# Feed-forward up products of a three-block kernel as 2x2 block products in seven multiplications, activations through DRAM

## Chip, core and metric

The kernel runs on one core of one Trainium2 chip. The metric is the device time of one execution in microseconds (us); the time of the kernel before is the median of three runs. All tensors are float32 in DRAM.

## The reference, cut to what matters

Three transformer blocks follow each other on 1024 tokens of width 1024. The first and the second end in a gated feed-forward of inner width 2816 (2730 padded up to a multiple of 256), and that is all the change touches.

```python
def first_block(x, ...):
    ...
    h = h + merged @ w_out[l]
    hn = rmsnorm(h, norm_ffn[l])
    g, up = jnp.split(hn @ w_ffn_in[l], 2, axis=-1)
    h = h + (jax.nn.silu(g) * up) @ w_ffn_out[l]
    return rmsnorm(h, norm_final)

def _hybrid_layer(x, p_i, ...):
    ...
    x = _layer_norm(ALPHA * x + mix, ln1_g, ln1_b)
    gate_ff, up_ff = jnp.split(x @ w_ffn_in, 2, axis=-1)
    ffn = (jax.nn.silu(gate_ff) * up_ff) @ w_ffn_out
    ple = jax.nn.sigmoid(x @ w_ple_gate) * (p_i @ w_ple_proj)
    return _layer_norm(ALPHA * x + ffn + ple, ln2_g, ln2_b)
```

## The kernel before

Every large product is made of three matmuls: a float32 operand is kept as two fp32r parts, hi (a rounded copy) and lo (the rest), and `mm3` (L89 to L95) issues hi by hi, hi by lo and lo by hi, each a 128x128 stationary block by 512 columns. `weight` (L78 to L88) brings one weight tile: SP starts the load of w_raw (128x1024, 512 KB), DVE casts w_hi (L86), POOL subtracts w_lo (L87).

`ffn` (L370 to L412) is called once in the first block ("ffn1") and once in the second ("ffn2"). The inner width is cut into F_TILES = 22 tiles of 128. `up(fi)` loads the gate and the up weights of a tile and makes, for each half of the tokens (hf, 512 columns), a gate product and an up product of 24 matmuls each (`fm`: 8 slices of the width by 3). ACT takes the Silu (L380), DVE multiplies (L381), ACT copies act_hi (L383), DVE subtracts act_lo (L384); the activations stay in SBUF. `down` (L387 to L397) adds, for a group of two tiles, their part of the down product to the residual h: for each of 8 token tiles t and 2 column halves n one PSUM tile of 2 x 3 = 6 matmuls, then a DVE addition into h (L395). The groups are nine of two and a last one of four (LAST = 4). The loop at L400 to L409 interleaves them: the first up tile of a group, the down products of the group before, the second up tile. With the last group the hook `done` runs the norm of each finished token tile and the start of the next block.

The order on each engine is that of the program text as a scheduler of the tile framework arranges it by priorities and buffer waits; a tile that gets a buffer waits for the last reader of what lay there. PSUM gives these products three tiles in turn: two tagged mm and one tagged mf; transposes have two more (tr). h is eight tiles of 128x1024 in SBUF through the whole feed-forward. x_fm are the inputs with the width on the partitions, hi and lo, for the two token halves; they lie in SBUF units of a ring (12 units in the first block; in the second one ring of 8 and one of 4). The norm that makes x_fm (L170 scales a row tile, PE transposes it at L156, ACT copies hi at L135, DVE subtracts lo at L137) is still at work on the second token half when the first feed-forward begins. In the second block a gated product ("ple") stands ahead of the feed-forward; DVE multiplies (L1040) and POOL adds it to h (L1042).

## Time and profile before

| | |
|---|---|
| median of three runs | 3527.93 us (3527.26 to 3531.14) |
| the profiled execution's own time | 3537.72 us |
| its span, first to last instruction | 3536.0 us |
| mean granted TensorE clock | 0.974 |
| PE busy | 3367.1 us (95%), 15456 matmuls and transposes in the records |
| DVE, ACT, POOL busy | 1896.1 (54%), 877.4 (25%), 1048.1 us (30%) |
| feed-forward stages | about 716 to 1463 us and 2118 to 2859 us |

The page is of one execution, so times of stretches are compared with 3537.72 us and not with the median. The names in it: PE is the matmul engine, PEld its weight loads, which run beside it, DVE the vector engine, ACT the scalar engine, POOL the GpSimd engine, SP the engine that issues most loads. A matmul's own row shows the time from its start to its modelled end, and matmuls overlap; how long one takes of PE's time is read from the number of them in a stretch. "[3.49 <-DVE hm L931]" behind a row is idle time of that engine just before it and what ended it.

### The profile page before, as it was taken

Reading aid. Unit: us, or ns where it says so; the run is one execution under the profiler, and the core shown is the slowest. Engines: PE = TensorE matmul, PEld = TensorE weight load, DVE = VectorE, ACT = ScalarE, POOL = GpSimd, SP = SyncE. Lnnn points to the kernel's source line nnn. Section 1 sums busy time; section 2 is a strip of 40 time slices with the busy share of each in tenths; the row PEclk is TensorE's granted clock in tenths of the full one; section 3 lists DMA queues with packets and bytes.
Section 4 is the critical chain, followed back from the end, with each engine's and each line's share of the span. In section 5 each row is a group of like instructions: output and inputs, shape, how many; then the busy total and the mean of one; then the engine's idle time right before and its main releaser. Section 6 shows DMA issues by size and latency. Waiting matters only on the chain. (4 is left out here: it accounts for less than half of the span.)

```text
span 3536.0 us, 39137 instructions
## 1 busy us (share of the span) xinstructions
PE 3367.1 (95%) x15456; PEld 2750.8 (78%) x15456; DVE 1896.1 (54%) x3048; ACT 877.4 (25%) x1694; POOL 1048.1 (30%) x618
## 2 busy tenths in 40 slices
PE   8999999999999999999979899999999986889998
PEld 6888888888888888778768788888888865667776
DVE  5455457343333333657768843334334379985665
ACT  3333311110000000312245520000000133445552
POOL 3111122132222222133444452222222366552221
PEclk9999999999999999999989999999999988999899
DMA  4111124221111111222251121111111221122241
GB/s 137 65 62 62 57 63 132 95 60 45 52 48 48 48 48 54 78 84 90 85 185 49 36 77 56 54 50 44 54 49 42 72 81 36 42 93 78 76 143 66
DMA packets 88359, 247.13 MB, mean 70 GB/s; under 512 B 13120, under 2 KB 18368, under 8 KB 88176
## 3 DMA queue, kind: packets, MB, share of 16 engines
q1 hardware_dynamic: 60176, 194.60, 17.4%
q10 hardware_dynamic: 27952, 49.91, 4.3%
q8 instruction: 121, 1.98, 0.2%
q14 instruction: 62, 0.51, 0.0%
q0 software_dynamic: 48, 0.13, 0.0%
HBM read 204.17 MB, written 40.69 MB: 69 GB/s over the span
## 5 line engine op out<-in xcount | busy, mean ns | idle before, releaser
L87 POOL TENSOR_TENSOR w_lo<-w_raw,w_hi 128x1024 fp32r<-128x1024 f32 x267 | 657.1, 2462 | 1891.1 <-DVE w_hi L86 1434.0
L86 DVE CAST w_hi<-w_raw 128x1024 fp32r<-128x1024 f32 x259 | 235.6, 910 | 468.6 <-PE mm L94 272.3
L93 PE MATMUL mm<-x,w_hi 128*128 128x512 f32 x696 | 284.5, 409 | 23.5 <-DVE kl L277 10.5
L94 PE MATMUL mm<-x,w_hi 128*128 128x512 f32 x696 | 283.2, 407 | 0.0
L95 PE MATMUL mm<-x,w_lo 128*128 128x512 f32 x696 | 280.5, 404 | 1.9 <-POOL w_lo L87 1.9
L93 PE MATMUL mf<-x,w_hi 128*128 128x512 f32 x568 | 229.1, 403 | 12.4 <-DVE u L1126 11.5
L95 PE MATMUL mf<-x,w_lo 128*128 128x512 f32 x568 | 225.2, 396 | 1.2 <-POOL w_lo L87 1.2
L94 PE MATMUL mf<-x,w_hi 128*128 128x512 f32 x568 | 225.8, 397 | 0.0
L395 DVE TENSOR_TENSOR h<-h,mm 128x512 f32<-128x512 f32 x210 | 143.9, 686 | 116.8 <-PE mm L95 116.5
L94 PE MATMUL mm<-h,w_hi 128*128 128x512 f32 x512 | 199.5, 390 | 0.2 <-DVE h L137 0.2
L93 PE MATMUL mm<-h,w_hi 128*128 128x512 f32 x512 | 199.4, 389 | 0.1
L95 PE MATMUL mm<-h,w_lo 128*128 128x512 f32 x512 | 199.2, 389 | 0.0
L93 PE MATMUL mm<-w_hi,act_hi 128*128 128x512 f32 x462 | 183.6, 398 | 0.0
L94 PE MATMUL mm<-w_lo,act_hi 128*128 128x512 f32 x462 | 182.9, 396 | 0.0
L95 PE MATMUL mm<-w_hi,act_lo 128*128 128x512 f32 x462 | 182.8, 396 | 0.0
L383 ACT ACTIVATE act_hi<-sg 128x512 fp32r<-128x512 f32 x88 | 55.7, 632 | 505.6 <-DVE sg L381 499.6
L93 PEld LDWEIGHTS mm<-x,w_hi 128*128 128x128 f32 x696 | 135.0, 194 | 57.1 <-issue 23.5
L95 PE MATMUL mm<-y,w_lo 128*128 128x512 f32 x448 | 174.3, 389 | 0.0
L94 PE MATMUL mm<-y,w_hi 128*128 128x512 f32 x448 | 174.3, 389 | 0.0
L93 PE MATMUL mm<-y,w_hi 128*128 128x512 f32 x448 | 174.3, 389 | 0.0
L381 DVE TENSOR_TENSOR sg<-sg,mm 128x512 f32<-128x512 f32 x64 | 43.7, 684 | 238.7 <-PE mm L95 237.5
L1140 DVE SCALAR_TENSOR_TENSOR cy<-u,cols,cy 128x1024 f32<-128x1024 f32 x80 | 166.2, 2083 | 0.9
(430 smaller groups left out, 7837.7 us busy)
## 6 DMA issues: line engine op xcount, KB each, us to landing
w_raw<-in_w_ffn_in_dram SPq DMA_DIRECT2D x88, 512.0 KB, 3.6
w_raw<-in_w_in_dram SPq DMA_DIRECT2D x78, 512.0 KB, 3.6
w_raw<-in_w_ffn_out_dram SPq DMA_DIRECT2D x44, 512.0 KB, 3.5
w_raw<-in_w_out_dram SPq DMA_DIRECT2D x24, 512.0 KB, 3.7
gates_d<-go SPq DMA_DIRECT2D x32, 256.0 KB, 2.0
gt<-gates_d ACTq DMA_DIRECT2D x32, 256.0 KB, 3.5
x_d<-h SPq DMA_DIRECT2D x16, 512.0 KB, 2.6
xt<-in_x_dram SPq DMA_DIRECT2D x8, 512.0 KB, 8.4
```

Source lines behind the costliest of these rows:

```text
L86: nc.vector.tensor_copy(hi, raw)
L87: nc.gpsimd.tensor_tensor(out=lo, in0=raw, in1=f(hi), op=ALU.subtract)
L93: mm(out_, lh, rh, start=start and i == 0, stop=False)
L94: mm(out_, lh, rl, start=False, stop=False)
L95: mm(out_, ll, rh, start=False, stop=stop and i == n - 1)
L381: tt(out=sg, in0=sg, in1=u, op=ALU.mult)
L383: act(out=at[0][:, c], in_=sg, func=AF.Copy)
L395: tt(out=h, in0=h, in1=pt, op=ALU.add)
L1140: stt(out=y, in0=src, scalar=w, in1=y, op0=ALU.mult, op1=ALU.add)
```

## The change

The up products and the down products are taken apart: all 22 up tiles come first, their activations (float32, before the split) go to a DRAM buffer act_d, and then all down products run, which load them again (L549), copy the hi part on ACT (L550) and subtract the lo part on DVE (L551). h is written to DRAM before the up products (ACT's queue, L532) and read again before the down products (ACT's queue, L570); the space of h is used by the pool "up" in between.

Twenty of the 22 up tiles are made as a 2x2 block product in seven multiplications. The four blocks of a weight tile pair are (gate, up) by (first, second half of the width); the four blocks of the input are (first, second half of the width) by (first, second half of the tokens). Each multiplication is four slices of the width by three matmuls, 12 matmuls, so a tile has 84 in place of 96. Seven weight operands per tile are prepared: three blocks as they are and four sums and differences (s1 on POOL, s2, s4, s3 on DVE, L462); ACT copies the hi part of each (L448), POOL subtracts the lo part (L449). They are prepared AHEAD = 6 operands ahead of their product. On the input's side t1, t3, t2 and a new b12 are made once per feed-forward (`sums`, `last_sums`; L391, L396, L402, L405, L407, L415). The results are put together on DVE (L507, L514, L515, L518, L523) from PSUM tiles pa, pd (the mm pair) and pb, pc (own banks, one buffer each). The first two tiles are made in the plain way, the second token half first, while `sums` runs in between.

In the first block the activations of the first groups are loaded into the same ring of 12 units that holds x_fm, t1 and t3; in the second into the ring of 4. The diff, cut (the calls in the two blocks pass the rings, a DRAM tile for h and a function that opens h's pool again):

```diff
-    def mm3(out_, terms, start=True, stop=True):
+    def mm3(out_, terms, start=True, stop=True, onto=False):
...
+    def silu_mul(pl, g, u, dst, c):
+        sg = pl.tile([P, HS], F32, name="sg", tag="sg", bufs=2)
+        act(out=sg, in_=g, func=AF.Silu)
+        tt(out=dst[:, c], in0=sg, in1=u, op=ALU.mult)
...
+    def ffn_up(pl, pp, unit, unit_r, x_fm, w_in, act_d, plain=2):
...
+        half_k = lambda h, k: tuple(fm_.at[4 * k][0] for fm_ in x_fm[h])
+        b11, b21, b12, b22 = half_k(0, 0), half_k(0, 1), half_k(1, 0), half_k(1, 1)
+        t1, t3 = (tuple(four(unit(f"{n}{j}")) for j in range(2)) for n in ("t1", "t3"))
+        t2 = tuple(four(unit_r(f"t2{j}")) for j in range(2))
+        dve, pool_e = nc.vector.tensor_tensor, nc.gpsimd.tensor_tensor
...
+        def whole(n, x, k, eng):
+            o = tmp(n)
+            eng(out=o, in0=f(x[0][:, k]), in1=f(x[1][:, k]), op=ALU.add)
+            return o
+        def parts(x, k, src, eng):
+            act(out=x[0][:, k], in_=src, func=AF.Copy)
+            eng(out=x[1][:, k], in0=src, in1=f(x[0][:, k]), op=ALU.subtract)
+        def sums():
+            for k in range(4):
+                x11, x12, x22 = whole("p1", b11, k, pool_e), whole("u2", b12, k, dve), whole("u3", b22, k, pool_e)
+                dve(out=x11, in0=x12, in1=x11, op=ALU.subtract)
+                parts(t1, k, x11, pool_e)
+                yield
+                dve(out=x12, in0=x22, in1=x12, op=ALU.subtract)
+                parts(t3, k, x12, pool_e)
+                dve(out=x22, in0=x22, in1=x11, op=ALU.subtract)
+                parts(t2, k, x22, dve)
+                yield
...
+        def last_sums():
+            for k in range(4):
+                x21, y2 = whole("p1", b21, k, pool_e), whole("u2", t2, k, dve)
+                dve(out=x21, in0=x21, in1=y2, op=ALU.subtract)
+                parts(b12, k, x21, pool_e)
...
+            return ao, lambda h: nc.sync.dma_start(act_d[fi][:, sl[h]], ao[:, sl[h]])
+        gen = sums()
+        for fi in range(plain):
             wg, wu = weight(w_in[fi]), weight(w_in[F_TILES + fi])
...
+            ao, store = out_of(fi)
+            for h in (1, 0):
+                g = fm(wg, x_fm[h])
+                u = fm(wu, x_fm[h])
+                silu_mul(pl, g, u, ao, sl[h])
+                store(h)
+                for _ in range(2 if fi < plain - 1 or h else 8):
+                    next(gen, None)
+        n_op, held = [0], []
...
+        def operand(src, eng):
+            hi, lo = slot()
+            nc.scalar.copy(hi, src)
+            eng(out=lo, in0=src, in1=f(hi), op=ALU.subtract)
+            return hi, lo
+        def operands(fi):
+            raw = []
+            for j in (F_TILES + fi, fi):
+                r = wp.tile([P, 1024], F32, name="w_raw", tag="w_raw", bufs=2)
+                nc.sync.dma_start(r, w_in[j])
+                raw.append(r)
+            (a21, a22), (a11, a12) = ((r[:, 0:512], r[:, 512:1024]) for r in raw)
+            def mix(x, y, op, eng):
+                s = pl.tile([P, 512], F32, name="s", tag="s", bufs=4)
+                eng(out=s, in0=x, in1=y, op=op)
+                return s
+            yield operand(a11, pool_e)
+            s1 = mix(a21, a22, ALU.add, pool_e)
+            yield operand(s1, pool_e)
+            s2 = mix(s1, a11, ALU.subtract, dve)
+            yield operand(s2, pool_e)
+            s4 = mix(a12, s2, ALU.subtract, dve)
+            s3 = mix(a11, a21, ALU.subtract, dve)
+            yield operand(a12, pool_e)
+            yield operand(s3, pool_e)
+            yield operand(a22, pool_e)
+            yield operand(s4, pool_e)
...
+        AHEAD = 6
+        xs = (b11, t1, t2, b21, t3, b12, b22)
...
+        more(AHEAD)
+        last_sums()
...
+            def product(i, pt, start=True):
+                w = ready.pop(0)
+                mm3(pt, [(kslice(w, k), tuple(x[:, k] for x in xs[i])) for k in range(4)], start, onto=not start)
+            pa, pd = mmtile("mm", 2), mmtile("mm", 2)
+            pb, pc = (pp.tile([P, HS], F32, name=n, tag=n, bufs=1) for n in ("pb", "pc"))
+            p1, u2, u3 = tmp("p1"), tmp("u2"), tmp("u3")
+            product(0, pa)
+            act(out=p1, in_=pa, func=AF.Copy)
+            more(1)
+            product(1, pc)
+            more(1)
+            product(2, pb)
+            tt(out=u2, in0=p1, in1=pb, op=ALU.add)
+            more(1)
+            product(3, pa, False)
+            sg = tmp("sg")
+            act(out=sg, in_=pa, func=AF.Silu)
+            more(1)
+            product(4, pb, False)
+            tt(out=u3, in0=p1, in1=pb, op=ALU.add)
+            tt(out=p1, in0=u3, in1=pc, op=ALU.add)
+            more(1)
+            product(5, pd)
+            tt(out=u3, in0=u3, in1=pd, op=ALU.add)
+            tt(out=ao[:, sl[0]], in0=sg, in1=u3, op=ALU.mult)
+            store(0)
+            more(1)
+            product(6, pc, False)
+            tt(out=u2, in0=u2, in1=pc, op=ALU.add)
+            act(out=u2, in_=u2, func=AF.Silu)
+            tt(out=ao[:, sl[1]], in0=u2, in1=p1, op=ALU.mult)
+            store(1)
+            more(1)
...
+    def ffn(x_fm, unit, unit_b, h, h_d, h_st, open_h, w_in, w_out, before_last, done, group=2):
+        act_d = dram.tile([F_TILES, P, S], F32, name="act_d")
+        for t in range(NT):
+            nc.scalar.dma_start(h_d[t * P:(t + 1) * P], h[t])
+        h_st.close()
+        with ExitStack() as c:
+            pool("up_edge", side="right", c=c).tile([P, 24], F32, name="edge")
+            unit_r = units(pool("up_t2", side="right", c=c), 2)
+            ffn_up(pool("up", side="right", c=c), pool("up_ps", space=PSUM, c=c), unit, unit_r, x_fm, w_in, act_d)
+        open_h()
+        with ExitStack() as c:
+            pool("down_edge", side="right", c=c).tile([P, 24], F32, name="edge")
+            dp = pool("down", side="right", c=c)
...
+            def load(fi, last):
+                if last:
+                    hi, lo = (dp.tile([P, S], F32R, name=f"act_{j}", tag=f"act_{j}", bufs=LAST) for j in ("hi", "lo"))
+                else:
+                    at = unit_b("act")
+                    hi, lo = at[:, 0:S], at[:, S:2 * S]
+                nc.sync.dma_start(f(lo), act_d[fi])
+                act(out=hi, in_=f(lo), func=AF.Copy)
+                nc.vector.tensor_tensor(out=lo, in0=f(lo), in1=f(hi), op=ALU.subtract)
+                return hi, lo
...
+            def down(fis, ats, done=None):
...
+                        pt = mmtile()
+                        mm3(pt, [(tuple(x[:, t * P:(t + 1) * P] for x in at), kslice(w, n, 512))
+                                 for at, w in zip(ats, ws)])
+                        hh = h[t][:, n * 512:(n + 1) * 512]
+                        tt(out=hh, in0=hh, in1=pt, op=ALU.add)
...
+            groups = [list(range(g, g + group)) for g in range(0, F_TILES - LAST, group)]
+            groups.append(list(range(F_TILES - LAST, F_TILES)))
+            ats = [[load(fi, False) for fi in groups[0]]]
             for t in range(NT):
...
+                nc.scalar.dma_start(h[t], h_d[t * P:(t + 1) * P])
+            for i, fis in enumerate(groups[:-1]):
+                nxt_g = groups[i + 1]
+                ats.append([load(fi, nxt_g is groups[-1]) for fi in nxt_g])
+                down(fis, ats[i])
+            before_last()
+            down(groups[-1], ats[-1], done)
+            done.flush()
```

PE at the start of the first feed-forward, before (mg is the merged input of the projection, h_5194 and h_5196 are hi and lo of the first token half, tr a transpose of the norm xn):

```order
3179 L94 MATMUL mm<-w_lo,mg_4547 128x512
3180 L95 MATMUL mm<-w_hi,mg_4549 128x512
3181 L93 MATMUL mf<-h_5194,w_hi 128x512 [waits DVE_49,Activation_49]
3182 L93 MATMUL mm<-h_5194,w_hi 128x512 [waits DVE_49]
3183 L156 MATMUL tr<-sq_c,xn 128x128 [waits DVE_49,PE_49]
3184 L156 MATMUL tr<-sq_c,xn 128x128 x3
3185 L94 MATMUL mf<-h_5196,w_hi 128x512
3186 L95 MATMUL mf<-h_5194,w_lo 128x512 [waits Pool_49]
```

The same place after (h_5198 is hi of the second token half):

```order
3193 L158 MATMUL tr<-sq_c,xn 128x128 [waits DVE_49]
3194 L158 MATMUL tr<-sq_c,xn 128x128 x3
3195 L158 MATMUL tr<-sq_c,xn 128x128 [waits DVE_49]
3196 L158 MATMUL tr<-sq_c,xn 128x128 x3
3197 L95 MATMUL mf<-h_5198,w_hi 128x512 [waits Activation_49]
3198 L95 MATMUL mm<-h_5198,w_hi 128x512
3199 L95 MATMUL mm<-h_5194,w_hi 128x512
3200 L96 MATMUL mm<-h_5196,w_hi 128x512
```

Up products of the first token half stood between the transposes of the second half; now the first product comes after all transposes, and is of the second half.

DVE after, where the first feed-forward goes from its last Strassen tile to the down products (L514 to L525 put that tile together, L551 are the lo parts of loaded activations, L562 the additions into h):

```order
957 L514 TENSOR_TENSOR u_8876<-p_8874,pb 128x512 [waits PE_49]
958 L551 TENSOR_TENSOR act<-act 128x1024 [waits DMAHW2_49,Activation_49]
959 L515 TENSOR_TENSOR p_8874<-u_8876,pc 128x512 [waits DVE_49]
960 L551 TENSOR_TENSOR act<-act 128x1024 [waits DMAHW3_49,Activation_49]
961 L518 TENSOR_TENSOR u_8876<-u_8876,mm 128x512 [waits DVE_49,PE_49]
962 L551 TENSOR_TENSOR act<-act 128x1024 [waits DMAHW4_49,Activation_49]
963 L519 TENSOR_TENSOR ao<-sg,u_8876 128x512 [waits DVE_49]
964 L551 TENSOR_TENSOR act<-act 128x1024 [waits DMAHW5_49,Activation_49]
965 L523 TENSOR_TENSOR u_8875<-u_8875,pc 128x512 [waits PE_49]
```

Nothing of before answers to it; there the additions into h stand between those of up tiles. Five more of L551 and L525 follow, then the first L562 (row 971).

ACT after, at the same place (L550 are the hi copies of loaded activations, L524 the last Silu, L570 the loads of h):

```order
649 L550 ACTIVATE act<-act 128x1024 [waits DMAHW6_49,PE_49]
650 L524 ACTIVATE u_8875<-u_8875 128x512 [waits DVE_49,Activation_49]
651 L550 ACTIVATE act<-act 128x1024 [waits DMAHW0_49,PE_49]
652 L550 ACTIVATE act<-act 128x1024 [waits DMAHW2_49,PE_49]
653 L550 ACTIVATE act<-act 128x1024 [waits DMAHW3_49,PE_49]
654 L570 DMA h_8983<-h_d 128x1024 [waits Pool_49]
655 L570 DMA h_8984<-h_d 128x1024 [waits DMAHW1_49]
```

The loads of h stand behind the copies of all activations that the ring of 12 takes. In all, PE's order of after has 480 matmuls less than that of before.

## Rows read from the trace of the kernel before

**Rows 1.** The page, engines: busy us (share of the span), instructions.
```profile
PE 3367.1 (95%) x15456; PEld 2750.8 (78%) x15456; DVE 1896.1 (54%) x3048; ACT 877.4 (25%) x1694; POOL 1048.1 (30%) x618
```

**Rows 2.** Stretches of both feed-forwards: length, busy per engine (instructions), clock, DMA share, GB/s.
```profile
800.00:900.00 100.00, 100.00 (x438) 81.97 (x438) 35.94 (x46) 7.38 (x12) 22.79 (x10) 1.00 0.16 48
...
1300.00:1400.00 100.00, 100.00 (x440) 82.25 (x439) 31.18 (x39) 8.89 (x15) 20.18 (x9) 1.00 0.15 43
...
2100.00:2200.00 100.00, 100.00 (x441) 82.27 (x440) 31.43 (x37) 11.06 (x17) 29.92 (x14) 1.00 0.18 53
...
2700.00:2800.00 100.00, 100.00 (x440) 82.23 (x439) 32.08 (x41) 8.61 (x14) 21.58 (x9) 1.00 0.19 60
```

**Rows 3.** Groups of instructions on feed-forward lines: busy us, mean ns, idle before.
```profile
L395 DVE TENSOR_TENSOR h<-h,mm 128x512 f32<-128x512 f32 x210 | 143.9, 686 | 116.8 <-PE mm L95 116.5
L383 ACT ACTIVATE act_hi<-sg 128x512 fp32r<-128x512 f32 x88 | 55.7, 632 | 505.6 <-DVE sg L381 499.6
```

**Rows 4.** Lines of POOL and DVE: minimum, median, maximum ns, first and last start.
```profile
L1042 POOL TENSOR_TENSOR h<-h,sg x16: 1282/1292/1735, 2045.6 to 2121.7; 128x512 f32<-128x512 f32 x16
L87 POOL TENSOR_TENSOR w_lo<-w_raw,w_hi x267: 2344/2397/3383, 22.9 to 3500.5; 128x1024 fp32r<-128x1024 f32 x134
L86 DVE CAST w_hi<-w_raw x259: 659/694/2822, 21.8 to 3499.7; 128x1024 fp32r<-128x1024 f32 x130
L384 DVE TENSOR_TENSOR act_lo<-sg,act_hi x88: 691/1144/1893, 736.5 to 2801.3; 128x512 fp32r<-128x512 f32 x88
```

**Rows 5.** DMA issues: count, KB each, median us from issue to landing.
```profile
w_raw<-in_w_ffn_in_dram SPq DMA_DIRECT2D x88, 512.0 KB, 3.6
...
x_d<-h SPq DMA_DIRECT2D x16, 512.0 KB, 2.6
...
h<-in_x_dram ACTq DMA_DIRECT2D x8, 512.0 KB, 7.8
```

**Rows 6.** Start us, duration us, instruction: a DVE operation beside one of POOL, and alone.
```profile
2993.70 3.36 DVE L1140 SCALAR_TENSOR_TENSOR cy<-u,cols,cy 128x1024 f32<-128x1024 f32 x1
...
2993.63 2.35 POOL L1146 TENSOR_TENSOR y<-y,pr 128x1024 f32<-128x1024 f32 x1 [1.26 <-ACT pr L1145]
...
3014.70 1.27 DVE L1140 SCALAR_TENSOR_TENSOR cy<-u,cols,cy 128x1024 f32<-128x1024 f32 x1
```

**Rows 7.** Start of the first feed-forward: a stretch, and two DVE rows.
```profile
720.00:740.00 20.00, 18.75 (x94) 14.92 (x93) 9.37 (x13) 6.59 (x10) 5.27 (x3) 1.00 0.23 72
...
717.24 0.67 DVE L581 TENSOR_TENSOR h<-h,mm 128x512 f32<-128x512 f32 x1
...
732.59 1.29 DVE L137 TENSOR_TENSOR h<-tr,h 128x512 fp32r<-128x512 f32 x2 [0.78 <-ACT h L135]
```

**Rows 8.** 128x1024 operations of ACT and DVE with SBUF operands: minimum, median, maximum ns.
```profile
L165 ACT ACTIVATE junk<-h x32: 1043/1060/1069, 682.9 to 3528.8; 128x1024 f32<-128x1024 f32 x32
...
L170 DVE SCALAR_TENSOR_TENSOR xn<-h,rstd,gain x8: 1272/1283/1287, 684.9 to 727.7; 128x1024 f32<-128x1024 f32 x8
```

**Rows 9.** PE after a gap in the second block, timeline, and the stretch's clock.
```profile
1748.73 0.77 PE L922 MATMUL co<-vt,W 128*128 128x129 f32 x2 [3.49 <-DVE hm L931]
...
1753.16 0.63 PE L94 MATMUL mf<-x,w_hi 128*128 128x512 f32 x1
1753.59 0.63 PE L95 MATMUL mf<-x,w_lo 128*128 128x512 f32 x1
...
1750.00:1755.00 5.00, 5.00 (x21) 4.55 (x21) 3.95 (x16) 2.09 (x8) 2.01 (x2) 0.55 0.29 112
```

**Rows 10.** A stretch at the program's start, when loads come in a burst.
```profile
10.00:12.00 2.00, 1.01 (x5) 1.01 (x6) 1.55 (x2) 1.15 (x2) 1.36 (x1) 1.00 1.07 415
```

More of the change, by code (lines that the diff above doesn't have):

```diff
@@ L559, in block1, with open_h @@
         att_stack.close()
-        hp_ = pool("h1", side="right", c=mp)
-        h = [hp_.tile([P, D], F32, name=f"h{t}") for t in range(NT)]
+        h, h_st = [], ExitStack()
+        def open_h(c=mp):
+            hp_ = pool("h1", side="right", c=c)
+            h[:] = [hp_.tile([P, D], F32, name=f"h{t}") for t in range(NT)]
+        open_h(h_st)
         h_fm = new_fm("h1")
@@ L596, in block1 @@
                       *(lambda t, fn=fn: fn(t, h[t], nxt[0], nxt[1][0]) for fn in finish))
-        with ExitStack() as c:
-            fp = pool("ffn1", side="right", c=c)
-            ffn(fp, h_fm, h, a["w_ffn_in"], a["w_ffn_out"], before_last, done)
+        ffn(h_fm, unit, unit, h, dram.tile([S, D], F32, name="h1_d"), h_st, open_h, a["w_ffn_in"], a["w_ffn_out"],
+            before_last, done)
         mp.close()
@@ L995, in block2, with open_h @@
         unit("low")
-        hp_ = pool("h2", side="right", c=hs)
-        h = [hp_.tile([P, D], F32, name=f"h{t}") for t in range(NT)]
+        h, h_st = [], ExitStack()
+        def open_h(c=hs):
+            hp_ = pool("h2", side="right", c=c)
+            h[:] = [hp_.tile([P, D], F32, name=f"h{t}") for t in range(NT)]
+        open_h(h_st)
         mix = gqa(unit, unitb, h, ple, at)
@@ L1045, in block2 @@
                       *(lambda t, fn=fn: fn(t, h[t], nxt[0], nxt[1][0]) for fn in finish))
-        with ExitStack() as c:
-            fp = pool("ffn2", side="right", c=c)
-            ffn(fp, x_fm, h, a["w_ffn_in_2"], a["w_ffn_out_2"], before_last, done)
+        ffn(x_fm, unit, unitb, h, dram.tile([S, D], F32, name="h2_d"), h_st, open_h, a["w_ffn_in_2"],
+            a["w_ffn_out_2"], before_last, done)
         hs.close()
```

72 lines of the change are left out of this document (33 added, 39 removed).

## Prediction

> **What bounds the kernel now.** I read the busy shares first, then the table of stretches, the rows of the feed-forward lines, and last the places where two engines meet. PE is busy 95% of the span; DVE, ACT and POOL have large gaps [rows 1]. Inside both feed-forward stages there is nothing but PE: each of four 100 us stretches shows PE at 100.00 with 438 to 441 matmuls at a granted clock of 1.00, while DVE has 31 to 36, ACT 7 to 11 and POOL 20 to 30 us of work in them [rows 2]. So one 128x512 matmul costs 100/438 = 0.228 us there, a matmul removed gives back 0.228 us, and whatever makes PE wait there is paid in full: no idle time in these stages can absorb it.
>
> **What is removed.** A plain up tile costs 4 products of 8 k-slices by 3 matmuls = 96 matmuls. A Strassen tile costs 7 products of 4 k-slices by 3 = 84. That is 12 less for 20 of 22 tiles in two feed-forwards: 480 matmuls, 480 x 0.228 = **109.4 us**, all of it on the path, since PE is the bound. The down products stay 1056 per feed-forward, and the rest of the program keeps its order but for small swaps. A gain beyond this I exclude inside the stages, since PE has no idle there to be recovered [rows 2]; every other term below is a loss or nothing.
>
> **Strassen, steady state.** One tile gives PE 84 x 0.228 = 19.2 us. ACT gets seven operand copies, one product copy and two Silu of 128x512, ten by 0.63 = 6.3 us [rows 3]. POOL gets seven subtractions and a sum, 8 x 1.29 = 10.3 us [rows 4]. DVE gets five operations that read PSUM and five with two SBUF inputs, ten by 0.69 = 6.9 us [rows 3]. The two weight loads of 3.6 us each [rows 5] have 19 us. So no engine but PE is full. The point to watch is order. Bank pb is written again by the third product of the next tile, but in PE's order one product (12 matmuls, 2.7 us) lies between its last matmul and that; L514 must have read it by then. For pc there are two products (5.5 us). The two-input operations on DVE do not keep to 0.69 us: beside a POOL operation a 128x1024 one took 3.36 us, and it ended 1.08 us after POOL's end, while the same line took 1.27 us with POOL idle [rows 6]; the 128x512 subtraction of L384 ranges from 691 to 1893 ns, median 1144 [rows 4]. I read this as: such an operation waits until POOL's running one ends. POOL works 10.3 of 19.2 us, so one operation of DVE is held 0.54 x 0.65 = 0.35 us on average, which 2.7 us of slack covers; at worst two of them stand ahead of L514, 2 x (1.29 + 0.69) + 0.69 = 4.7 us, 1.9 us late. Bounds for 40 tiles: 0 and 76 us; near the mean, 0.15 us each, **6 us**.
>
> The Trainium skill ("SBUF — State Buffer", section "Who interferes with whom") says that VectorE and GpSimd share a port pair, that an instruction of VectorE with two SBUF inputs contends with a GpSimd instruction that reads SBUF, and that the later one is blocked for the whole of the earlier one. The 3.36 us beside 1.27 us agree [rows 6]. The rule speaks against this change, which puts more such work on both; by its letter the slower rival below is the outcome, by the rows' mean the forecast.
>
> **Entry to Strassen.** Before product t2 of the first Strassen tile, the sums of the input blocks (t1, t3, t2 and the new b12) need 28 two-input operations on DVE, 24 on POOL and 16 copies on ACT, besides 4 casts and 4 subtractions for the two plain tiles and 7 or so POOL operations for the first operands. POOL: 24 x 1.29 + 4 x 2.40 + 7 x 1.29 = 49.6 us [rows 4]; DVE: 28 x 0.69 + 4 x 0.69 + 2 = 24 us. PE covers it with two plain tiles, 192 x 0.228 = 43.8 us, and two first products, some 5.5: 49. If the two engines worked side by side, POOL would just fit (about 0 to 3 us lost). If they exclude each other, it is 74 against 49: 25 us lost, and part of it comes early, since the multiplication L375 that frees the second PSUM tile of the plain products stands behind 20 sums on DVE. The rows lie between; I take **11 us** for each feed-forward, bounds 2 and 25.
>
> The first feed-forward loses more. Before, the products of token half 0 fill PE while the norms of half 1 are finished: the last projection add starts at 717.24, the last norm operation at 732.59, and PE is busy 18.75 of 20 us between 720 and 740 [rows 7]. After, the plain tile begins with half 1, and PE's order has only transposes ahead of it. From the last projection add (717.24) the norm needs the square sum 1.06, the scaling 1.28 [rows 8], two transposes with a copy and a subtraction each: to about 724. That is some **7 us** idle (5 to 17, if it stays as late as 732.6), and PE comes back at half clock: after a 3.49 us gap at 1748.73 the matmuls stand 0.43 us apart for some 5.5 us, granted clock 0.55 [rows 9], about **2 us** lost. Storing h (2.6 us a tile [rows 5], burst 415 GB/s [rows 10]) also has to end before the tiles laid over it are written; eight are 4 MB, 10 us of burst, beside the plain products. Entry: 20 us (6 to 44) and 12 us (2 to 27).
>
> **Exit to the down products, first feed-forward.** DVE's and ACT's orders decide this. PE, after its last product but one, has two down tiles (12 matmuls, 2.7 us) and then waits for pc, freed by L515, which stands behind L551 of an activation whose unit comes free only with a matmul just before. Load 3.6 [rows 5], copy 1.06, subtraction 1.28 [rows 8], L515 0.69: 6.6, so 3.9 us idle. After the last product PE can fill one more tile or so (1.4 us); the first addition into h is queued behind all remaining act subtractions, and the reload of h is queued on ACT behind their copies. Seven loads, 3.6 + 6 x 1.3 (512 KB at about 400 GB/s [rows 10]) = 11.4, copy 1.06, load of h 3.6, add 0.69: 16.8, less 1.4 = 15.4 us idle. With two slow starts of 2 us and weights in the same SP queue (two loads, 2.6 us), with L551 held by POOL once or twice (up to 2.4 us each): **28 us**, bounds 18 (no collision) and 42 (loads at 7.8 us, as in a burst of eight [rows 5]).
>
> **Exit, second feed-forward.** Only four act units are free early, so the reload of h follows the last Silu: 0.69 + 0.63 + 3.6 + 0.69 = 5.6, less 1.4, then the slow start; the second add waits behind a subtraction L551 whose load shares the queues with eight loads of h. **12 us**, bounds 5 and 22.
>
> **Down products.** A group of two is 96 matmuls, 21.9 us; DVE has 16 adds (11.0 us), two casts (0.69 to 2.8, [rows 4]) and two L551 (1.28 alone, 3.36 beside POOL [rows 6]). Three PSUM tiles give DVE 2 x 1.37 = 2.7 us of delay; one L551 held by POOL costs about 0.6 us more than that. Some ten groups have L551: **12 us**, bounds 0 and 25. The loads are 2 MB in 21.9 us, about 96 GB/s against bursts of 415 [rows 10]: nothing.
>
> **The sum.** 20 + 12 + 28 + 12 + 12 + 6 = 90 us of loss against 109.4 of gain: -19.4 us. The profiled execution took 3537.72 us and would be 3518; the median of the runs lies 9.8 us below it, so 3527.9 - 19.4 = **3508 us**. Lower ends together: 6 + 2 + 18 + 5 = 31 (3449 us). Upper ends: 44 + 27 + 42 + 22 + 25 + 76 = 236 (3655 us), which don't come together.
>
> **Rivals.**
> - *The ends cost little (3450 us).* The norms of half 1 finish early, loads land in 1.3 us one after another, and POOL and DVE overlap: all at the lower ends, 31 us. For it speaks that DMA is nearly idle [rows 2]; against it the orders, in which h is reloaded last.
> - *The gain is just eaten (3530 us).* Exits at their upper ends, 42 + 22 instead of 40: 90 + 24 = 114. It needs loads at 7.8 us instead of 3.6, as the eight loads at the start show [rows 5].
> - *Slower: DVE's queue holds PSUM (3590 us).* Operations that read pb and pc stand behind two-input operations held by POOL; at 1.9 us a tile it is 76 instead of 6, and the two entries lose 17 each instead of 11: 90 + 82 = 172, +62 us. For it: 3.36 beside 1.27 [rows 6]. Against it: POOL is busy only half of a tile, and one product lies between. It decides the sign from 0.6 us per tile on: (6 + 19.4) / 40.
> - *The products aren't saved.* The order shows 480 matmuls less, so no chance.
>
> **How the numbers follow.** The forecast 0.48 (own range 3485 to 3521), little cost 0.17, just eaten 0.15, slower 0.20. About 0.2% (7 us) is what a measurement can tell: faster 0.48 + 0.17 = 0.65, same 0.15, slower 0.20. The range leaves out half of the slower case and a third of the cheap one: 3455 to 3570 us.
>
> **What would show it.** PE with 480 matmuls less and 0.228 us each; in a Strassen stretch PE above 98 of 100 with some 438 matmuls (right) or below 92, waiting for DVE L514 or L515 (the slower rival); PE idle after the last projection matmul and again near the end of the two plain tiles; at the end of the first up phase two gaps, about 4 and 15 us, the second released by an add into h whose load came last on ACT; a smaller one in the second; two or so us of clock below 1.00 after each. Wrong would be: no gap at the exits, a stretch of Strassen with PE idle in each tile, or down stretches below 97 of 100.

## The result: 31 us faster, and the profile after

The changed kernel takes 3498.51 us (median of four runs, 3493.91 to 3509.02) where the kernel before takes 3529.53 (3527.26 to 3532.18): a ratio of 0.9916, 95% interval 0.9892 to 0.9940, or 21 to 38 us. The forecast was 3508 us, 19 us less than before. The profiled execution took 3509.02 us against 3537.72, 28.7 us less; the sums below are made against these two.

The page of the changed kernel, engines (busy us, share of the span, instructions), beside [rows 1]:

```profile
PE 3278.3 (93%) x14976; PEld 2674.0 (76%) x14976; DVE 2169.9 (62%) x3300; ACT 1066.3 (30%) x2002; POOL 1368.6 (39%) x906
```

PE has exactly 480 instructions less, and it is busy for 88.8 us less. The span shrank by only 28.7 us, so PE idles some 60 us more than before. DVE has 274 and POOL 320 us more to do.

Where the time went is read from three operations that both kernels have, the landmarks of what follows: the last scaling of the first block's final norm, the first POOL addition of the gated product ahead of the second feed-forward (2045.6 in [rows 4]), and the first scaling in the third block. Before, minimum, median and maximum ns, first and last start:

```profile
L170 DVE SCALAR_TENSOR_TENSOR h<-h,rstd,gain x8: 1273/1275/1285, 1414.6 to 1459.5; 128x1024 f32<-128x1024 f32 x8
...
L170 DVE SCALAR_TENSOR_TENSOR xn<-h,rstd,g x2: 1276/1277/1278, 2873.6 to 2879.5; 128x1024 f32<-128x1024 f32 x2
```

After:

```profile
L172 DVE SCALAR_TENSOR_TENSOR h<-h,rstd,gain x8: 1274/1277/1286, 1400.0 to 1444.0; 128x1024 f32<-128x1024 f32 x8
...
L172 DVE SCALAR_TENSOR_TENSOR xn<-h,rstd,g x2: 1279/1282/1284, 2844.3 to 2849.8; 128x1024 f32<-128x1024 f32 x2
...
L1216 POOL TENSOR_TENSOR h<-h,sg x16: 1281/1292/1745, 2033.7 to 2110.4; 128x512 f32<-128x512 f32 x16
```

The first feed-forward ends 15.5 us earlier (1444.0 against 1459.5). The stretch between the two loses 4 us again (the gated product starts 11.9 us earlier, 2033.7 against 2045.6). From there to the third block another 17.4 us are gained (29.3 in all), and the rest loses about 1.

A stretch of Strassen tiles (those made in seven multiplications), beside [rows 2] (length, busy us and instructions of PE, PEld, DVE, ACT, POOL, clock, DMA share, GB/s):

```profile
2300.00:2400.00 100.00, 100.00 (x443) 82.84 (x442) 45.48 (x54) 29.23 (x52) 54.30 (x41) 1.00 0.25 82
```

PE is full, here and from 860 to 960 us, with 443 matmuls where the stretches before, which mix up and down products, had 438 to 441. A stretch of plain tiles alone, from the first experiment below, has 443 too, so the steady state costs nothing:

```profile
2200.00:2300.00 100.00, 100.00 (x443) 82.80 (x442) 12.67 (x19) 5.39 (x9) 21.60 (x9) 1.00 0.23 76
```

What PE waits for at the ends of the first up phase (total us, times, longest), first its start, 700 to 820 us:

```profile
PE tr L158 <- DVE h L139: 3.7, 3, 2.5
PE pb L95 <- DVE u L514: 3.6, 1, 3.6
PE mm L95 <- DVE ao L375: 3.4, 1, 3.4
PE tr L158 <- DVE rstd L148: 2.7, 1, 2.7
PE mm L95 <- ACT p L502: 1.0, 1, 1.0
```

and its end, 1150 to 1220 us:

```profile
PE mm L95 <- DVE h L562: 11.9, 2, 11.3
PE pc L95 <- DVE p L515: 3.5, 1, 3.5
```

The first and fourth line of the start are the transposes of the norms of the second token half, which PE now waits for with nothing between. The third, L375, stands behind the sums on DVE. L514 and L502 stand behind operations on weights that came late; on DVE, just ahead of L514:

```profile
803.53 0.69 DVE L462 TENSOR_TENSOR s<-s,w_raw 128x512 f32<-128x512 f32 x1 [10.57 <-DMA w_raw<-in_w_ffn_in_dram]
```

SP could issue these loads (at 783.9 and 799.9 us) only when POOL had let go a buffer of w_raw, so they too belong to the start of Strassen, but to its first operands. At the end stand the two gaps of the prediction, behind L515 and behind the addition into h. The rows around the second, DVE:

```profile
1168.72 3.06 DVE L551 TENSOR_TENSOR act<-act 128x1024 fp32r<-128x1024 f32 x1
1171.70 0.67 DVE L515 TENSOR_TENSOR p<-u,pc 128x512 f32<-128x512 f32 x1
...
1184.19 1.23 DVE L551 TENSOR_TENSOR act<-act 128x1024 fp32r<-128x1024 f32 x1 [0.44 <-ACT act L550]
1189.80 0.69 DVE L562 TENSOR_TENSOR h<-h,mm 128x512 f32<-128x512 f32 x1 [4.38 <-DMA h<-h_d]
```

POOL beside the first of these:

```profile
1168.33 2.36 POOL L87 TENSOR_TENSOR w_lo<-w_raw,w_hi 128x1024 fp32r<-128x1024 f32 x1 [0.68 <-DVE w_hi L86]
```

and ACT, with its queue of issued loads:

```profile
1183.10 1.06 ACT L550 ACTIVATE act<-act 128x1024 fp32r<-128x1024 f32 x1 [0.61 <-DMA act<-act_d]
1183.12 9.22 ACTq L570 DMA_DIRECT2D h<-h_d  x8
```

L515 had to wait for an L551 that took 3.06 us beside POOL's L87, where others take 1.2. The loads of h left ACT only with the last copy of a loaded activation, at 1183.12, and the first addition into h came 6.7 us later. The last two loads of activations ahead of them had been issued only at 1177.5, when the last product let go their units; DMA moved nothing from 1176 to 1178 us.

At the second feed-forward, 2060 to 2200 us:

```profile
PE mm L96 <- POOL y L396: 7.0, 2, 4.1
PE mf L95 <- DVE ao L375: 2.8, 1, 2.8
PE mm L97 <- POOL w_lo L449: 1.0, 1, 1.0
PE mm L95 <- ACT y L395: 0.6, 1, 0.6
```

The sums end last there: the lo parts of the new b12 on POOL (L396).

### The profile page after: what moved, and what is told of

It is laid out like the page before. It is cut to its first block, busy times and chain, and to the rows that moved or that the text cites. A ratio compares the mean times of both kernels' runs of the same rounds, so it can differ in the third digit from the quotient of the medians.

```text
span 3507.3 us, 40024 instructions
## 1 busy us (share of the span) xinstructions
PE 3278.3 (93%) x14976; PEld 2674.0 (76%) x14976; DVE 2169.9 (62%) x3300; ACT 1066.3 (30%) x2002; POOL 1368.6 (39%) x906
## 5 line engine op out<-in xcount | busy, mean ns | idle before, releaser
L87 POOL TENSOR_TENSOR w_lo<-w_raw,w_hi 128x1024 fp32r<-128x1024 f32 x187 | 467.1, 2499 | 1224.7 <-DVE w_hi L86 888.3
L449 POOL TENSOR_TENSOR w_lo<-s,w_hi 128x512 fp32r<-128x512 f32 x160 | 220.4, 1385 | 113.6 <-ACT w_hi L448 112.1
L449 POOL TENSOR_TENSOR w_lo<-w_raw,w_hi 128x512 fp32r<-128x512 f32 x120 | 166.7, 1389 | 106.8 <-ACT w_hi L448 106.8
L562 DVE TENSOR_TENSOR h<-h,mm 128x512 f32<-128x512 f32 x214 | 145.0, 683 | 96.8 <-PE mm L97 88.6
L514 DVE TENSOR_TENSOR u<-p,pb 128x512 f32<-128x512 f32 x40 | 27.5, 687 | 267.1 <-PE pb L97 267.1
L95 PE MATMUL mm<-w_hi,act 128*128 128x512 f32 x384 | 153.6, 400 | 25.4 <-DVE h L562 24.9
L95 PEld LDWEIGHTS mm<-x,w_hi 128*128 128x128 f32 x688 | 132.2, 192 | 55.4 <-issue 24.0
L448 ACT CAST w_hi<-s 128x512 fp32r<-128x512 f32 x160 | 97.3, 619 | 236.5 <-PE pc L96 152.2
L97 PEld LDWEIGHTS mm<-x,w_lo 128*128 128x128 f32 x688 | 131.8, 192 | 28.9 <-issue 1.5
L96 PEld LDWEIGHTS mm<-x,w_hi 128*128 128x128 f32 x688 | 132.3, 192 | 27.0 <-issue 2.0
L96 PE MATMUL mm<-w_lo,act 128*128 128x512 f32 x384 | 151.4, 394 | 0.0
L97 PE MATMUL mm<-w_hi,act 128*128 128x512 f32 x384 | 151.2, 394 | 0.0
L335 ACT ACTIVATE st<-st,nmax 128x128 f32<-128x128 f32 (+5 forms) x192 | 119.3, 623 | 104.0 <-DVE nmax L329 99.5
L95 PEld LDWEIGHTS mf<-x,w_hi 128*128 128x128 f32 x576 | 110.9, 192 | 41.1 <-DVE u L1299 14.9
```

Source lines behind the costliest of these rows:

```text
L87: nc.gpsimd.tensor_tensor(out=lo, in0=raw, in1=f(hi), op=ALU.subtract)
L95: mm(out_, lh, rh, start=start and i == 0, stop=False, **kw)
L96: mm(out_, lh, rl, start=False, stop=False, **kw)
L97: mm(out_, ll, rh, start=False, stop=stop and i == n - 1, **kw)
L335: act(out=st[:, :w + extra], in_=st[:, :w + extra], func=AF.Exp, scale=-1.0, bias=nmax, accum_out=ssum)
L448: nc.scalar.copy(hi, src)
```

## Experiments

Three questions had to be settled: what the gain of 109 us was spent on (the split of up and down, or Strassen's own operands), what the waits at the ends come from (work that excludes work on another engine, the order on an engine, or transfers), and why one row of the down products is not explained by any wait.

Each run's ratio is to the kernel before on the same chip, where the median of that was 3529.5 to 3535.0 us. The chips differ, so a difference to the changed kernel is given from the medians and, behind it, from the two ratios; the second is uncertain by some 11 us.

### All tiles plain

```diff
-    def ffn_up(pl, pp, unit, unit_r, x_fm, w_in, act_d, plain=2):
+    def ffn_up(pl, pp, unit, unit_r, x_fm, w_in, act_d, plain=F_TILES):
...
-        gen = sums()
+        gen = iter(())
...
-        more(AHEAD)
-        last_sums()
```

> All 22 up tiles are made in the plain way (no sums, no operands, 96 matmuls a tile); up and down products stay apart, activations and h still go through DRAM. Theory A, the terms of the forecast hold: against the changed kernel it gains 0 and pays 480 matmuls x 0.227 = 109 us, and gets back what the sums cost at the two entries (about 11 us in the first feed-forward, 18 in the second, read from the changed kernel's idle PE): 3498 + 109 - 29 = 3578 us, some 48 us slower than the kernel before, and that is the price of taking up and down apart. Rival B, the split costs nothing and Strassen itself loses half of its gain in its own operands: 3530 us, equal to the kernel before. By A PE in the plain stretches stays at 100 and the two gaps at the exits stay.

Measured (e1): 3562.54 us (3559.75 to 3563.94), ratio to before 1.0080 (1.0063 to 1.0097). The split alone makes the kernel slower, as theory A said, but Strassen brings 64 us of its 109 (58 by the ratios) and not 80: its own operands and sums cost 45 us or more and not 29. The waits for sums and first operands (13 and 18 us with the slow clock after them) make up 31; the rest lies at the ends of the up phases, where in this kernel PE has no wait for L515 and its longest wait for an addition into h is 8.0 and 4.5 us.

### The kernel before, shifted by 96 bytes

In the two traces one row is not explained by any wait. In each down group of two PE has nothing but down products for 22 us, with no gap, at clock 1.00. In the kernel before, 20 us of one (length, busy us and instructions of PE, PEld, DVE, ACT, POOL, clock, DMA share, GB/s):

```profile
788.00:808.00 20.00, 20.00 (x87) 16.07 (x86) 11.80 (x17) 0.63 (x1) 2.40 (x1) 1.00 0.11 33
```

In the changed kernel:

```profile
1300.00:1320.00 20.00, 20.00 (x90) 16.52 (x89) 12.68 (x17) 0.00 (x0) 4.81 (x2) 1.00 0.16 54
```

87 matmuls before, 90 after, of the same form. By the starts of successive matmuls it is 0.2343 us before and 0.2272 after; all up products and all others take 0.2267 in both. The edit, for both feed-forwards of the kernel before:

```diff
+            pool("ffn1_edge", side="right", c=c).tile([P, 24], F32, name="edge")
             fp = pool("ffn1", side="right", c=c)
```

> The kernel before, with one unused tile of 24 floats per partition (96 bytes) ahead of the feed-forward's pool, so that the activations lie 96 bytes further on; nothing else. In the kernel before, matmuls of the down products follow each other at 0.2343 us, in the changed kernel at 0.2272, all others at 0.2267 in both. Theory A, the place of the activations in SBUF makes it: 0.2267 here and 2112 x 0.007 = 15 us less, 3514 us. Rival B, the mixing of up and down products makes it: 0.2343 and 3529 us as before.

Measured (e2): 3516.81 us (3516.34 to 3517.32), ratio 0.9953 (0.9938 to 0.9968). The same stretch there:

```profile
787.00:807.00 20.00, 20.00 (x90) 16.57 (x89) 11.83 (x17) 0.63 (x1) 2.40 (x1) 1.00 0.09 31
```

90 again: 0.2267 us. An unused tile of 96 bytes makes the kernel before 15 us faster, with no other instruction changed. The changed kernel's down products follow each other as fast (0.2272), and so do those of all tiles plain (90 in 1300 to 1320 us). So 15 us of the change's 31 come from faster down products, which need no Strassen, and the place of the activations in SBUF is enough to give them. The diff of the change has the same 96 bytes ahead of its pools ("up_edge" and "down_edge"); no run takes them out of the changed kernel, so what they do there, where most activations lie in the ring of units, is not shown.

### The kernel before, shifted by 128 bytes

The same edit with [P, 32].

> The kernel before with 128 bytes per partition ahead of the feed-forward's pool, in place of the 96 of e2. Theory A, any shift of the activations against the weights does it: matmuls of the down products at 0.2267 us as in e2, 3516 us. Rival B, only certain offsets do, and a multiple of 128 bytes leaves things as they were: 0.2343 us and 3530 us.

Measured (e12): 3530.30 us (3525.87 to 3538.30), ratio 0.9992 (0.9979 to 1.0006).

```profile
786.00:806.00 20.00, 20.00 (x87) 16.05 (x86) 11.88 (x17) 0.63 (x1) 2.41 (x1) 1.00 0.10 33
```

87: it isn't any shift that helps. Which offsets do, and which of the two operands has to lie how to the other, stays open.

### The sums on DVE

```diff
-                x11, x12, x22 = whole("p1", b11, k, pool_e), whole("u2", b12, k, dve), whole("u3", b22, k, pool_e)
+                x11, x12, x22 = whole("p1", b11, k, dve), whole("u2", b12, k, dve), whole("u3", b22, k, dve)
...
-                parts(t1, k, x11, pool_e)
+                parts(t1, k, x11, dve)
```

and so for t3, b21 and b12. Why this tells the theories apart is seen in the changed kernel's entry, where both engines are busy without a break. DVE:

```profile
2128.38 1.77 DVE L396 TENSOR_TENSOR t<-u,t 128x512 fp32r<-128x512 f32 x1
2130.08 1.77 DVE L407 TENSOR_TENSOR u<-u,p 128x512 f32<-128x512 f32 x1
```

and POOL:

```profile
2127.87 1.74 POOL L396 TENSOR_TENSOR t<-u,t 128x512 fp32r<-128x512 f32 x1
2129.56 1.74 POOL L396 TENSOR_TENSOR t<-p,t 128x512 fp32r<-128x512 f32 x1
```

Each engine starts one operation every 1.70 us, where alone it would take 0.69 or 1.28. They take turns; a pair costs 1.70, a little less than the 1.97 of both in a row.

> The changed kernel with all sums of the input blocks on DVE (24 operations moved from POOL); the rest as it is. Theory A, a DVE operation with two SBUF inputs and a POOL operation exclude each other (a pair takes 1.70 us in the changed kernel's trace, 0.69 and 1.28 alone): the entry's work falls from about 74 to 55 us and PE's waits for sums shrink by half, some 8 us in each feed-forward: 3483 us (3476 to 3492). Rival B, they run side by side: DVE alone then needs 52 x 0.69 = 36 us where it had 20, the multiplication that frees the plain products' PSUM comes later, and the kernel is 5 to 10 us slower: 3505 us.

Measured (e3): 3488.70 us (3479.11 to 3493.41), ratio 0.9870 (0.9848 to 0.9891): 10 us less than the changed kernel (16 by the ratios), in the direction of A. The first feed-forward became 7 us shorter and lost its wait for L375; the second gained only 2, since there L375 and L502 still wait, 3.5 and 4.0 us, behind a longer row of sums on DVE.

### The first token half first

```diff
-            for h in (1, 0):
+            for h in (0, 1):
...
-                for _ in range(2 if fi < plain - 1 or h else 8):
+                for _ in range(2 if fi < plain - 1 or not h else 8):
```

> The changed kernel with the two token halves of the plain tiles in the other order, the first half first; the sums' steps follow the second half as before. Theory A: the 9 us that PE loses beside the norms of the second half (6.5 idle, 2.6 of slow transposes) are filled with products: 8 us less, 3490 us. Rival B: the sums need both halves and start no earlier, so that the same time is lost a little later, at the multiplication behind the sums: 3497 us.

Measured (e4): 3502.27 us (3496.04 to 3505.70), ratio 0.9910 (0.9893 to 0.9926), not to be told from the changed kernel. By the landmarks the first feed-forward is 5 us shorter and the stretch up to the third block 6.6 longer. In the first, PE's waits for transposes fell from 6.4 to 1.7 us, but those for the sums and first operands grew from 8.0 to 12.5, so that it waits as long as before; what differs is the granted clock beside the norms, 1.00 from 715 to 740 us where the changed kernel has 0.50 to 0.60 from 720 to 735. In the second, the waits for sums grew from 11.4 to 16.8:

```profile
PE mm L95 <- ACT y L395: 5.5, 1, 5.5
PE mm L96 <- POOL y L396: 5.3, 2, 5.0
PE mm L95 <- DVE ao L375: 3.2, 2, 1.8
PE mf L95 <- DVE ao L375: 2.8, 1, 2.8
```

By the waits rival B holds in both feed-forwards; the 5 us of the first go with the clock, since only there PE had transposes alone to do.

### Three plain tiles

```diff
-    def ffn_up(pl, pp, unit, unit_r, x_fm, w_in, act_d, plain=2):
+    def ffn_up(pl, pp, unit, unit_r, x_fm, w_in, act_d, plain=3):
```

> The changed kernel with three plain tiles in place of two, so that the sums have 21.8 us more of products beside them, for 12 matmuls more in each feed-forward (2 x 2.7 us). Theory A, PE waits at the entries because the work of DVE and POOL is longer than its cover: most of the 11 and 18 us come back, 3498 + 5 - 22 = 3481 us. Rival B, the waits come from the order on DVE (a multiplication behind 20 sums) and from the latency of the chain: they stay, 3503 us.

Measured (e7): 3499.16 us (3497.93 to 3499.87), ratio 0.9895 (0.9876 to 0.9914), not to be told from the changed kernel: nearer to B by the medians, and B by the waits. In the first feed-forward PE's waits for sums and first operands fell from 8.0 to 5.1 us, in the second they went from 11.4 to 13.9:

```profile
PE mm L95 <- DVE ao L375: 6.5, 1, 6.5
PE pb L95 <- DVE u L514: 4.4, 1, 4.4
PE mm L95 <- ACT p L502: 3.0, 1, 3.0
```

More cover didn't help here: L375, L502 and L514 read PSUM, and PE still waits for them. The edit leaves the eight steps of the sums beside the first two tiles, so that it tests cover for the last sums and the operands, not a looser spacing of the sums.

### The weight sums twice

```diff
-                eng(out=s, in0=x, in1=y, op=op)
+                for _ in range(2 if eng is dve else 1):
+                    eng(out=s, in0=x, in1=y, op=op)
```

> The changed kernel with the three sums and differences of the weights on DVE (L462) made twice: eight operations with two SBUF inputs in a Strassen tile in place of five. It tests the slower rival of the prediction. If such operations hold back the reading of PSUM as that rival said, each tile loses 1 to 2 us more, 40 to 80 us in all: 3540 to 3580 us. If PE's slack of one product covers them, as no wait of PE in the Strassen stretches says, only the entries lose a little: 3498 to 3504 us.

Measured (e8): 3554.97 us (3545.44 to 3565.03), ratio 1.0054 (1.0032 to 1.0075), 56 us more than the changed kernel (49 by the ratios): 1.2 to 1.4 us a tile. The expectation of the slower rival, not of my forecast. A Strassen stretch, beside the row 2300 to 2400 above:

```profile
2300.00:2400.00 100.00, 94.75 (x408) 76.94 (x407) 60.19 (x65) 26.97 (x47) 54.67 (x39) 0.98 0.26 78
```

DVE at one tile (lines lie one further on in this kernel, L524 is L523 of the changed one), then PE:

```profile
1001.11 2.47 DVE L463 TENSOR_TENSOR s<-s,w_raw 128x512 f32<-128x512 f32 x2 [3.85 <-DMA w_raw<-in_w_ffn_in_dram]
1003.68 1.60 DVE L463 TENSOR_TENSOR s<-w_raw,s 128x512 f32<-128x512 f32 x1
1005.21 1.78 DVE L463 TENSOR_TENSOR s<-w_raw 128x512 f32<-128x512 f32 x1
1006.91 0.68 DVE L463 TENSOR_TENSOR s<-w_raw,s 128x512 f32<-128x512 f32 x1
1007.51 0.68 DVE L463 TENSOR_TENSOR s<-w_raw 128x512 f32<-128x512 f32 x1
1008.11 0.67 DVE L524 TENSOR_TENSOR u<-u,pc 128x512 f32<-128x512 f32 x1
...
1008.84 0.50 PE L95 MATMUL pc<-t,w_hi 128*128 128x512 f32 x1 [1.87 <-DVE u L524]
```

Six operand operations come in a row when the weights land and take 7.0 us, because three of them take 1.6 to 1.8 us beside POOL where they take 0.7 alone; L524, which frees pc, comes only at 1008.11, and PE's next product into pc starts 1.87 us late. DVE is 60% busy in such a stretch: it isn't full, it is late. So the slower rival's mechanism is real, and the changed kernel stands at most three operations away from it.

### The loads of h from POOL's queue

```diff
-                nc.scalar.dma_start(h[t], h_d[t * P:(t + 1) * P])
+                nc.gpsimd.dma_start(h[t], h_d[t * P:(t + 1) * P])
```

> The changed kernel with the loads of h issued by POOL in place of ACT, where they stand behind the last copy of a loaded activation. Theory A, the place in ACT's order sets the first exit (first load of h issued at 1183.1, first addition at 1189.8, last L551 done at 1185.4): the gap of 11.3 us shrinks by the 4.4 us between these, and by some 3 us at the second exit: 3491 us. Rival B, the transfers set it: DMA moves 400 GB/s from 1172 to 1195 us, an earlier load of h makes the activations later by as much: 3498 us.

Measured (e6): 3515.17 us (3511.41 to 3519.31), ratio 0.9941 (0.9920 to 0.9962): 17 us more than the changed kernel, 9 by the ratios, which is within their uncertainty; the gain of theory A didn't come. The longest wait for an addition into h became 16.2 and 16.1 us at the two exits. The eight loads, 1150 to 1220 us:

```profile
h<-h_d POOLq DMA_DIRECT2D x8, 512.0 KB, 10.9
```

The first was issued at 1170.2 us, the other seven from 1177.3 on, six us earlier than from ACT. The first tile of h landed at 1176.9, where it landed at 1189.8 in the changed kernel. What then stood ahead of the first addition is seen on DVE:

```profile
1190.68 1.23 DVE L551 TENSOR_TENSOR act_lo<-act_lo,act_hi 128x1024 fp32r<-128x1024 f32 x1 [5.02 <-ACT act_hi L550]
1193.31 1.23 DVE L551 TENSOR_TENSOR act_lo<-act_lo,act_hi 128x1024 fp32r<-128x1024 f32 x1 [1.41 <-ACT act_hi L550]
1194.45 0.68 DVE L562 TENSOR_TENSOR h<-h,mm 128x512 f32<-128x512 f32 x1
```

In the changed kernel two additions stand ahead of the first of these L551. Here the edit changed DVE's order too: two lo parts of the last group come first, and their loads, now behind those of h, landed only from 1189.6 on. So h came 13 us earlier and the wait moved to the activations. That they come later by an earlier load of h is what rival B said; but since DVE's order moved with it, the run doesn't decide between the place in ACT's order and the transfers.

### The lo parts of the activations on POOL

```diff
-                nc.vector.tensor_tensor(out=lo, in0=f(lo), in1=f(hi), op=ALU.subtract)
+                nc.gpsimd.tensor_tensor(out=lo, in0=f(lo), in1=f(hi), op=ALU.subtract)
```

> The changed kernel with the lo parts of the loaded activations (L551, 44 operations of 128x1024) on POOL in place of DVE. Theory A: in the down stretches PE waits about 1 us in a group because an L551 stands among the additions into h, and at the first exit L515 stands behind one; without them on DVE some 11 us in the stretches and 3 to 4 us at the exit come back: 3485 us. Rival B: the additions wait for PE and not the other way round, or POOL's 2.4 us make the activations late: 3498 us.

Measured (e5): 3486.77 us (3480.08 to 3490.89), ratio 0.9864 (0.9840 to 0.9888), 12 us less than the changed kernel (18 by the ratios), as A said. A down stretch of the changed kernel:

```profile
1240.00:1260.00 20.00, 19.32 (x84) 15.36 (x83) 14.02 (x18) 0.44 (x1) 2.45 (x2) 1.00 0.18 60
```

and of this one:

```profile
1240.00:1260.00 20.00, 20.00 (x90) 16.52 (x89) 12.94 (x17) 2.13 (x2) 7.78 (x4) 1.00 0.25 86
```

By PE's starts the down stretches lose 9 us less, and the second exit 5. At the first exit the two waits are now 1.3 and 15.8 us, in sum 17.1 where they were 15.4: with L515 early, PE waits longer for h.

### Together, and with less loaded ahead of h

Both edits that helped:

> The edits of e3 (sums of the inputs on DVE) and e5 (lo parts of the loaded activations on POOL) together. They act at different places, the entries and the down stretches. Theory A: they add, 3498.5 - 10 - 12 = 3477 us. Rival B: some of it was only run to run spread (the changed kernel's runs lie 15 us apart) and the sum is less, 3485 us.

Measured (e9): 3472.06 us (3468.09 to 3475.51), ratio 0.9830 (0.9809 to 0.9850). They add, 26 us where the two alone gave 10 and 12 (30, 16 and 18 by the ratios).

Then, in the first feed-forward, eight units of the ring are taken by unused tiles behind the loads of the second group, until the sixth, so that only four activations are loaded ahead of h; it costs 16 small operations on POOL:

```diff
+                if i == 0 and unit_b is unit:
+                    held = [unit(f"held{j}") for j in range(8)]
+                    for x in held:
+                        nc.gpsimd.memset(f(x[:, 0:1]), 0.0)
...
+                if i == 5:
+                    for x in held:
+                        nc.gpsimd.tensor_tensor(out=scr, in0=f(x[:, 0:1]), in1=h[7][:, 0:1], op=ALU.add)
```

> e9, and in the first feed-forward only four activations are loaded ahead of h, as the second does it (eight units of the ring are held by unused tiles until the sixth group). Theory A, learned from the run with POOL's queue: at the first exit the transfers ahead of h set the gap (DMA is 95% busy there), eight loads of 512 KB at 1.3 us less: the gap goes from 17 us towards the 8 us of the second exit, 3468 us against e9's 3477. Rival B: the loads of h wait for the last Silu in any case, the gap stays, and the eight loads come back in the stretch after it: 3477 us.

Measured (e10): 3468.05 us (3464.07 to 3475.61), ratio 0.9815 (0.9790 to 0.9839). The waits at the first exit went from 1.4 and 16.2 us to

```profile
PE mm L95 <- DVE h L562: 6.6, 1, 6.6
PE pc L95 <- DVE p L515: 4.8, 1, 4.8
```

6 us less in all; the time is 4 us less, which the runs don't tell from nothing. The loads of h were issued hardly earlier, first without this edit and then with it:

```profile
1170.78 8.55 ACTq L570 DMA_DIRECT2D h<-h_d  x8
...
1170.14 12.77 ACTq L570 DMA_DIRECT2D h<-h_d  x8
```

With it they stand right behind the last Silu (L524, at 1170.06 us), as rival B said, and the first landed at 1176.4 against 1177.4. So that fewer transfers ahead of h shorten the gap is not shown.

Last, e10 with the token halves turned in the first feed-forward only:

> e10, and in the first feed-forward alone the plain tiles take the first token half first (e4 did it in both: 5 us better in the first, 6.6 us worse in the second). Theory A: the first feed-forward gains 5 us of the 9 beside the norms, also with the sums on DVE: 3463 us against e10's 3468. Rival B: with all sums on DVE the multiplication that frees PSUM stands behind the norm's work and more sums, and it is 3 us slower than e10.

Measured (e11): 3469.26 us (3465.70 to 3471.35), ratio 0.9821 (0.9801 to 0.9841), no different from e10. These three versions beat both kernels, the kernel before by some 60 us.

## Why the prediction was right, and where not

The direction and the order of size were right, and the time lies in the range. The table takes the terms of the sum, in us of the profiled executions; the runs are called by their labels. For the entries and exits it has PE's gaps and the time lost at the lower clock behind them (granted 0.59 from 1170 to 1175 us and 0.52 from 1190 to 1195, say), from the starts of its matmuls:

| term | forecast | measured |
|---|---|---|
| 480 matmuls removed | -109.4 | -108.8 (0.2267 each) |
| Strassen, steady state | 6 | 0 |
| entry, first feed-forward | 20 | 22, of it 9 the norms and 13 the sums and first operands |
| entry, second | 12 | 18 |
| exit, first | 28 | 20 |
| exit, second | 12 | 15 |
| down stretches | 12 | 11 (3 and 8) |
| sum of losses | 90 | 86 |
| faster down products | excluded | -15 |

- **The step that failed** is the sentence "A gain beyond this I exclude inside the stages, since PE has no idle there to be recovered". PE has no idle there, but 0.228 us was a mean of two rates, 0.2267 for up and 0.2343 for down products, and the change made the second the first. 2112 x 0.0071 = 15 us, shown by e2 without any Strassen. The 96 bytes stood in the diff and got no term in the sum. Without the faster down products the kernel would be 16 us faster by the medians, near the 19 of the forecast.
- That the losses came to 86 against 90 is luck in part: the terms missed by up to 8 us each, on both sides.
- By the table it should be 38 us faster and is 28.7 (31 by the medians). Four of the 9 us between are the stretch between the feed-forwards, where nothing was changed; over the profiled executions of all these kernels it takes 582 to 590 us. I found no cause for the rest.
- **Steady state**: right that PE's slack covers DVE's delays, and no wait is seen. But the forecast was right by less than it seemed: three more operations a tile cost 1.2 to 1.4 us (e8). The rival said that it decides the sign from 0.6 us a tile on; e8 has twice that and is slower than the kernel before. The rule of the Trainium skill that the prediction weighs ("SBUF — State Buffer", section "Who interferes with whom") agrees in kind with the pairs at 1.70 us, though full turns would make 1.97.
- **Entry**: the mechanism was right, norms first and sums then. The sums were sized at 11 in each; 13 and 18 (with the clock) were measured, and of the 8.0 us of waits in the first only the 3.4 behind L375 are the sums themselves, 4.6 the first operands. In the second feed-forward it is POOL that ends last. Taking the sums off POOL helped in the first (e3), more cover hardly (e7). The norms' 9 us are not all new: before, PE is idle for 1.25 us at the same place [rows 7].
- **First exit**: the two gaps were put at 4 and 15 us and were 3.5 and 11.3, and "the second released by an add into h whose load came last on ACT" is what the trace shows. The size was off because not seven loads stood ahead of h after the last product but two; they waited for their units, with DMA idle, so that the 400 GB/s from 1172 to 1195 us, as an expectation above has it, held only until 1174 and again from 1182 us on. What would shorten the gap stays open: e6 brought h 13 us earlier and the wait moved to the activations, e10 took transfers away and h came no earlier than by 1 us.
- **Second exit**: the parts given for it make 5.6 - 1.4 + 2 = 6.2 us, and 12 was taken; 15 were measured, so half of the term had no number behind it.
- **Down products**: sized 12, measured 11, and the cause, L551 among the additions into h, is confirmed by e5, which gave 9 of it back.
- The loss by the split itself is 46 us, from e1 against e2 (3562.5 - 3516.8), both with the down products at 0.227 us. The forecast's terms for it (norms, exits, down) made 61.

## To carry to other kernels

A full engine isn't an engine at its best rate: before a stretch is called bound, count its instructions by kind and compare the time of one across kinds. An operand stage cost the bound engine nothing here with three operations ahead of PSUM's readers on DVE's queue, and over 1 us a tile with six, at 45% and 60% busy; count the row that stands there, not the busy share. And where two phases are taken apart and state goes through DRAM, the price is at the seam: 20 and 15 us here. List what the first instruction of the new phase stands behind on every queue; with one load moved forward (e6), it waited for the next in the list.

## What the hardware showed unexpectedly

- The place of a tile in SBUF changed the rate of matmuls with no other change: 0.2343 us for 128x512 with the activations where they lay, 0.2267 with 96 bytes ahead of them, 0.2333 with 128 bytes. The granted clock was 1.00 in all three.
- A DVE operation with two SBUF inputs (0.69 us alone) and a POOL operation (1.28 alone) that run against each other take 1.70 us a pair, not 1.97 and not 1.28.
- Eight 512 KB loads of h, issued by POOL within 10 us beside loads of activations, landed 6.8 to 17.4 us after their issue, with DMA at 410 GB/s in between; loads of that size take 3.6 us in the median elsewhere [rows 5].
